# Strassen's weight sums cut into 256 KB chunks, one with each weight piece, and one difference of weights taken on VectorE

## The chip, the cores and the metric

The kernel runs on one core of a Trainium2 chip, as one launch. The metric is the device time of that launch in microseconds, the median of several runs. The core has five engines with instruction streams of their own: TensorE (PE, matrix products), VectorE (DVE), ScalarE (ACT), GpSimd (POOL) and SyncE (SP). Transfers between DRAM and the on-chip memory are issued by SP, ACT and POOL and carried out by 16 DMA engines that all queues share. An engine works its stream in order; an instruction that waits on a semaphore holds up those behind it on the same engine.

## The reference

A two-layer backbone over 256 latent tokens and 256 context tokens of width 2048: first a bidirectional retention layer, then a windowed attention layer, each behind an RMS norm and a modulation ("adaLN") computed from the conditioning vector. The change touches the end of the retention layer and what is prepared for it:

```python
def project(h):
    p = h @ w_in
    q = _heads(p[..., :RET_QK_W], RET_HEADS, RET_DK).astype(jnp.float32) * (RET_DK ** -0.5)
    k = _heads(p[..., RET_QK_W:2 * RET_QK_W], RET_HEADS, RET_DK).astype(jnp.float32)
    v = _heads(p[..., 2 * RET_QK_W:2 * RET_QK_W + RET_V_W], RET_HEADS, RET_DV).astype(jnp.float32)
    g = p[..., 2 * RET_QK_W + RET_V_W:]
    return q, k, v, g

def finish(o, g):
    b, h, l, dv = o.shape
    on = o * lax.rsqrt(jnp.mean(o * o, axis=-1, keepdims=True) + EPS)
    on = on.transpose(0, 2, 1, 3).reshape(b, l, h * dv) * norm_gain.astype(jnp.float32)
    return (on.astype(g.dtype) * jax.nn.silu(g)) @ w_out
```

`w_in` has 2048 x 12288 elements and `w_out` 4096 x 2048, all float32.

## The kernel before

**Precision.** A float32 operand is split into a high half, rounded to the matmul's type, and a low half, the rest. For a weight piece of 512 KB (128 partitions x 1024), `split_w` casts the raw tile `wraw` to `wh` on ScalarE (line 132) and subtracts on VectorE to get `wl` (line 113). The rings of `wraw`, `wh` and `wl` have three buffers each. `mm3` (lines 140 to 142) multiplies high by high, high by low and low by high: 24 matmuls of 512 columns for a piece.

**Stages.** Up to about 150 us the adaLN vectors of the first part and the normed inputs are made. Then come the eight heads (to about 1280 us): for each head the gate, query/key and value products with 24 weight pieces in all, loaded by SP, with the score and output products of a head, its decay table `dd` (a power on GpSimd, L761), its squares (`ossq`, L814), its `rs` (L241) and the sums `ue` of its result (L828) worked in between. The finished head's parts go to DRAM as `uB_d` by transfers issued on ScalarE (L832, L834). The output projection `@ w_out` follows as one level of Strassen's method: seven products of half size, M4 and M1 in one stage (about 1270 to 1385 us), then M5, M7, M2, M3 and M6 (to about 1630 us). The attention layer ends at 2050 us.

**Strassen's weights.** M5, M7, M2 and M3/M6 need sums of two quarters of `w_out` or a quarter itself. The four sums (`SUMS`) are made in DRAM, in the buffer `wS_d`, while the heads run: a job copies 1 MB of the first quarter to `wS_d` (L317, issued on ScalarE), and the step after it adds 1 MB of the second quarter by an accumulating transfer (L323, issued on GpSimd in packets of 4 KB). In front of each accumulating transfer stands the "pin", a copy of one column of the newest `wl` into `pin_t` (L321): GpSimd waits there until that `wl` is made, which fixes when the transfer starts, and the pin holds that `wl` buffer until it has run. `tc.issue_after(x)` places what it encloses behind the instruction x in the issue order. There are 32 jobs, four sums of 4 MB by parts of 1 MB with one more step at the end. `hook()` runs after each weight piece of the heads and takes a step at certain pieces only: its condition on `n`, the count of pieces from 1 to 168, gives six steps up to n = 32 (12, 14, 16, 28, 30, 32), then five in each 24 pieces (four of them two pieces apart, one ten pieces on), and the rest from n = 163.

**adaLN loads.** From n = 33 each hook also takes two adaLN steps (`ADAN`): SP loads 256 KB (`abraw`, four buffers), and VectorE multiplies and sums it with the conditioning rows (`ajunk`, L696), one or two instructions per load.

**M4 and M1.** M4 takes the quarter `wo0[1,1]`, M1 the difference `wo0[0,0] - wo0[1,1]`, which isn't among the sums. `weights1` makes it piece by piece: it loads b, splits it, writes -b into a second raw tile on ScalarE (L1014), and adds the other quarter to that tile by an accumulating transfer issued on GpSimd (L1015); then it splits the tile. In these stages the raw tiles rotate through seven buffers. `merged` (L960, L961) takes a finished product from PSUM into `x1` on ScalarE and VectorE, `prep` loads the next operands back from `uB_d`.

Of the kernel before, what the change touches and what calls it, by code (L numbers as in the profile page):

```python
# [13 lines left out]
AF = mybir.ActivationFunctionType  # L14
ALU = mybir.AluOpType
# [36 lines left out]
def backbone(ctx: ExitStack, tc, xT_d, w0_d, wo0_d, w1_d, wo1_d, adaS_d, adaB_d,  # L52
             crow_d, vec_d, cst_d, ropeR_d, ropeA_d, out_d, dbg=None):
    nc = tc.nc
# [74 lines left out]
    def split_w(raw):  # L129
        wh = strm.tile([P, 2, 512], F32R, name="wh", tag="wh", bufs=3)  # L130
        wl = strm.tile([P, 2, 512], F32R, name="wl", tag="wl", bufs=3)
        last_hi[0] = nc.scalar.copy(wh, raw).ins  # L132
        last_lo[0] = sub(wl, raw, wh).ins
        last_wl[0] = wl
        return wh, wl
# [8 lines left out]
    def gemm_ws(w_d, chunk, nkp, moving, n, hook=None, pre=None, tail=1):  # L144


        accs = [acc_tile()[:, :n] for _ in range(4)]
        w = {}
        for kp in range(nkp):
            if pre is not None:  # L150
                pre(kp)
            w[kp] = load_w(w_d[chunk, kp])
            if kp < nkp - tail:
                kps = [kp]
            elif kp < nkp - 1:
                continue
            else:
                kps = range(nkp - tail, nkp)
            for j in range(4):
                for kb in [2 * k + k2 for k in kps for k2 in range(2)]:  # L160
                    wh, wl = w[kb // 2]
                    js = slice(j * P, (j + 1) * P)
                    mm3(accs[j], (wh[:, kb % 2, js], wl[:, kb % 2, js]), moving(kb),
                        start=(kb == 0), stop=(kb == 2 * nkp - 1))
            if hook is not None:
                hook()
        return accs

    def gemm_ws2(w_d, chunk, nkp, s, hook=None, pre=None, tail=1):
# [4 lines left out]
        for kp in range(nkp):  # L174
            if pre is not None:
                pre(kp)
            w[kp] = load_w(w_d[chunk, kp])
            if nkp - tail <= kp < nkp - 1:
                continue
            kps = [kp] if kp < nkp - 1 else list(range(nkp - tail, nkp))  # L180

            def passes(js_, lo):
                for j in js_:
                    js = slice(j * P, (j + 1) * P)
                    for kb in [2 * k + k2 for k in kps for k2 in range(2)]:
                        wk = w[kb // 2][lo][:, kb % 2, js]
                        if lo:
                            nc.tensor.matmul(accs[j][:, 0:L], lhsT=wk, rhs=h1(kb, s)[:, 0],  # L188
                                             start=False, stop=(kb == 2 * nkp - 1))
                        else:  # L190
                            nc.tensor.matmul(accs[j], lhsT=wk, rhs=h1(kb, s).rearrange("p a t -> p (a t)"),  # L191
                                             start=(kb == 0), stop=False)


            for js_ in ([range(4)] if kp < nkp - 1 else [[j] for j in range(4)]):
                for lo in range(2):
                    passes(js_, lo)
            if hook is not None:
                hook()
        return accs  # L200

    def gemm_ts(w_d, chunk, nkp, stat, ntok, hook=None, pre=None):

        accs = [acc_tile() for _ in range(ntok)]
        for kp in range(nkp):
            if pre is not None:
                pre(kp)
            wh, wl = load_w(w_d[chunk, kp])
            for t in range(ntok):
                for k2 in range(2):  # L210
                    kb = 2 * kp + k2
                    mm3(accs[t], stat(kb, t), (wh[:, k2, :], wl[:, k2, :]),
                        start=(kb == 0), stop=(kb == 2 * nkp - 1))
            if hook is not None:
                hook()
        return accs
# [82 lines left out]
    def pump(n=1):  # L299
        for _ in range(n):  # L300
            if tasks and getattr(tasks[0], "need", None) not in missing:
                tasks.pop(0)()
# [5 lines left out]
    wS_d = dram.tile([4, 4, 4, P, 4, 256], F32, name="wS_d")  # L308
    SUMS = (((1, 0), (1, 1)), ((1, 0), (0, 0)), ((0, 0), (0, 1)), ((0, 1), (1, 1)))

    def sum_jobs():
        todo = [(i, r, slice(2 * q, 2 * q + 2)) for i in (2, 3, 0, 1) for r in range(4) for q in range(2)]
        for n in range(len(todo) + 1):
            if n < len(todo):
                i, r, q = todo[n]
                with tc.issue_after(last_hi[0]):
                    nc.scalar.dma_start(out=wS_d[i, r, q], in_=wo0_d[(*SUMS[i][0], r, q)])  # L317
            if n:
                i, r, q = todo[n - 1]

                pin = nc.gpsimd.tensor_copy(pin_t, last_wl[0][:, 0, 0:1].bitcast(F32)).ins  # L321
                with tc.issue_after(pin):
                    nc.gpsimd.dma_start(out=wS_d[i, r, q], in_=wo0_d[(*SUMS[i][1], r, q)], accum_op=ALU.add,  # L323
                                        max_dma_last_dim=4096)
            yield
    x1_d = dram.tile([KB, P, L], F32, name="x1_d")
# [331 lines left out]
    def raw_tile():  # L658
        i = ring[ring_n[0] % len(ring)]
        ring_n[0] += 1  # L660
        if i is None:
            return strm.tile([P, 2, 512], F32, name="wraw", tag="wraw", bufs=3)
        n, i = i
        return (r1 if n == "H" else top["pool"]).tile([P, 2, 512], F32, name="wraw",
                                                      tag=f"hl{i}" if n == "H" else f"t{i}")
# [9 lines left out]
    if True:  # L675
# [4 lines left out]
        def ada_jobs():  # L680
# [26 lines left out]
            open_top("wx")  # L707

        jobs, sums = ada_jobs(), sum_jobs()
        state = {"n": 0}  # L710

        def hook():
            state["n"] += 1
            n = state["n"]

            if n in (12, 14, 16, 28, 30, 32) or 32 < n < 161 and (n - 33) % 24 in (8, 10, 12, 14, 22) or n > 162:
                next(sums, None)
            if state["n"] > 32:
                with tc.issue_after(last_lo[0]):
                    for _ in range(ADAN[(state["n"] - 33) % 24 // 8]):  # L720
                        next(jobs, None)
            pump()
# [200 lines left out]
    with tc.tile_pool(name="pc", bufs=1, side="right") as pc:  # L923
# [9 lines left out]
        def quarter(src, r, kq):  # L933
            t = raw_tile()
            nc.sync.dma_start(out=t.rearrange("p a t -> p (a t)"),
                              in_=src[r, kq].rearrange("p k c -> p (k c)"))
            return t

        def comb(out, a, b, op):
            return nc.vector.tensor_tensor(out=out, in0=a, in1=b, op=op)  # L940
# [68 lines left out]


        def weights1(r, kq):
            b, a = quarter(wo0_d[1, 1], r, kq), raw_tile()
            yield split_w(b)
            nc.scalar.activation(a, b, AF.Copy, scale=-1.0)  # L1014
            nc.gpsimd.dma_start(out=a.rearrange("p a t -> p (a t)"),  # L1015
                                in_=wo0_d[0, 0, r, kq].rearrange("p k c -> p (k c)"), accum_op=ALU.add)
            yield split_w(a)

        def done1(r, m, accs, n1, n2):
# [37 lines left out]
        def hook_m2(r, kq):  # L1057
            if kq == 1:
                prep(M6, two(r))
            if kq == 2:  # L1060
                residual(two(r + 3), 0)

        stage((M4, M1), weights1, done1, hook1)
        single(M5, wS_d[2], done_m5, hook_m5)
        single(M7, wS_d[3], done_m7, hook_m7)
# [86 lines left out]
    with tc.tile_pool(name="pe", bufs=1, side="right") as pe:  # L1152
# [143 lines left out]
        for ch in ORDER:  # L1296
            c = int(ch[1])
# [128 lines left out]
```

## Time and profile before

| | us |
|---|---|
| median of 3 runs | 2042.59 |
| the runs | 2042.2 to 2047.46 |
| the profiled execution | 2052.4 |
| its span | 2050.6 |
| TensorE busy | 1970.6 |
| VectorE busy | 1323.2 |
| ScalarE busy | 771.4 |
| GpSimd busy | 387.3 |

The mean granted TensorE clock of that execution is 0.985 of full speed. In the rows of the profile an arrow out<-in names a tile written and the tile read; "x32" is a count; a bracket behind a timeline row gives the time the engine stood idle before the instruction and what ended it; "PEld" are TensorE's weight loads; SPq and POOLq are the issuing side of an engine. In a row by stretch the granted clock stands behind the engines' busy times, then the mean busy share of the 16 DMA engines and the GB/s.

### The profile page before, as it was taken

How to read it: one execution, taken by the hardware profiler on the slowest of the kernel's cores; microseconds unless marked ns; L12 is line 12 of the kernel's file. 1: busy time of each engine (PE TensorE's matmuls, PEld its weight loads, DVE VectorE, ACT ScalarE, POOL GpSimd, SP SyncE). 2: the span in 40 equal slices, each digit the busy share in tenths (PEclk: the TensorE clock that was granted, in tenths of full speed). 3: DMA queues.
4: the chain of work that ended last, by engine and by line, in shares of the span. 5: the costliest groups of instructions: out<-in, count | busy, mean ns of one | idle time of the engine just before them, and what ended most of it. 6: DMA issues, size and time to landing. Idle time of an engine off the chain costs nothing. (4 is left out here: it accounts for less than half of the span.)

```text
span 2050.6 us, 26254 instructions
## 1 busy us (share of the span) xinstructions
PE 1970.6 (96%) x9589; PEld 1626.8 (79%) x9589; DVE 1323.2 (65%) x2502; ACT 771.4 (38%) x1147; POOL 387.3 (19%) x207
## 2 busy tenths in 40 slices
PE   6999999999999989999989999979999999999999
PEld 3678787878878877878878878768888888888888
DVE  5575223869859858868547643547778854777765
ACT  4243222223223223223213234445555533666653
POOL 0226524303303302503400201210000010000001
PEclk9999999999999999999999999989999999999999
DMA  9953647797697696697697456768777334444455
GB/s 377 411 202 113 165 144 209 236 305 233 205 305 226 207 304 210 207 302 236 207 312 236 165 157 178 166 151 277 268 245 239 132 108 138 149 134 145 144 188 171
DMA packets 149825, 436.15 MB, mean 213 GB/s; under 512 B 15104, under 2 KB 37952, under 8 KB 145472
## 3 DMA queue, kind: packets, MB, share of 16 engines
q1 hardware_dynamic: 118800, 338.49, 48.5%
q0 software_dynamic: 11008, 41.95, 10.9%
q10 hardware_dynamic: 19888, 54.04, 7.4%
q8 instruction: 75, 1.23, 0.2%
q14 instruction: 54, 0.44, 0.1%
HBM read 416.04 MB, written 85.49 MB: 245 GB/s over the span
## 5 line engine op out<-in xcount | busy, mean ns | idle before, releaser
L113 DVE TENSOR_TENSOR wl<-wraw,wh 128x1024 fp32r<-128x1024 f32 x416 | 510.7, 1232 | 365.5 <-ACT wh L132 355.5
L132 ACT CAST wh<-wraw 128x1024 fp32r<-128x1024 f32 x415 | 433.1, 1050 | 792.6 <-DMA wraw<-in_w 182.9
L696 DVE SCALAR_TENSOR_TENSOR ajunk<-abraw,crow 128x512 bf16<-128x512 f32 x448 | 342.3, 764 | 127.5 <-DMA abraw<-in_adaB 118.8
L142 PE MATMUL acc<-hT_h,wl 128*128 128x512 f32 x928 | 368.2, 397 | 22.0 <-DVE wl L113 22.0
L140 PE MATMUL acc<-hT_h,wh 128*128 128x512 f32 x928 | 367.8, 396 | 6.5 <-ACT wh L132 6.5
L141 PE MATMUL acc<-hl,wh 128*128 128x512 f32 x928 | 365.8, 394 | 0.0
L142 PE MATMUL acc<-wh,hl 128*128 128x512 f32 x704 | 275.9, 392 | 0.0
L140 PE MATMUL acc<-wh,hT_h 128*128 128x512 f32 x576 | 224.6, 393 | 5.8 <-ACT wh L132 3.0
L141 PE MATMUL acc<-wl,hT_h 128*128 128x512 f32 x576 | 226.2, 393 | 3.6 <-DVE wl L113 3.6
L142 PEld LDWEIGHTS acc<-hT_h,wl 128*128 128x128 f32 x928 | 177.2, 191 | 65.2 <-DVE wl L113 27.8
L140 PEld LDWEIGHTS acc<-hT_h,wh 128*128 128x128 f32 x928 | 177.4, 191 | 44.6 <-ACT wh L132 7.8
L141 PEld LDWEIGHTS acc<-hl,wh 128*128 128x128 f32 x928 | 177.0, 191 | 36.2
L761 POOL TENSOR_TENSOR dd<-two,dd 128x128 f32<-128x128 f32 x8 | 168.3, 21038 | 92.0 <-DVE dd L759 92.0
L142 PEld LDWEIGHTS acc<-wh,hl 128*128 128x128 f32 x704 | 132.9, 189 | 27.8
L241 POOL TENSOR_TENSOR rs<-ms,mhalf 128x4 f32<-128x4 f32 (+1 forms) x23 | 32.1, 1397 | 558.4 <-DVE ms L235 310.6
L140 PEld LDWEIGHTS acc<-wh,hT_h 128*128 128x128 f32 x576 | 108.7, 189 | 31.6 <-issue 5.7
L141 PEld LDWEIGHTS acc<-wl,hT_h 128*128 128x128 f32 x576 | 109.0, 189 | 26.9 <-DVE wl L113 5.0
L321 POOL COPY pin_t<-wl 128x1 f32<-128x1 f32 x32 | 16.4, 513 | 472.2 <-DVE wl L113 472.2
L955 PE MATMUL acc<-r_h,wh 128*128 128x512 f32 x240 | 69.4, 420 | 15.2 <-ACT wh L132 10.8
L828 POOL TENSOR_TENSOR ue<-sg 128x512 f32<-128x512 f32 x38 | 66.3, 1759 | 77.9 <-DVE sg L818 44.3
L140 PE MATMUL acc<-wh,hl 128*128 128x512 f32 x192 | 75.4, 393 | 0.0
L141 PE MATMUL acc<-wl,hl 128*128 128x512 f32 x192 | 74.8, 389 | 0.0
(265 smaller groups left out, 2855.3 us busy)
## 6 DMA issues: line engine op xcount, KB each, us to landing
wraw<-in_w SPq DMA_DIRECT2D x272, 512.0 KB, 4.2
abraw<-in_adaB SPq DMA_DIRECT2D x256, 256.0 KB, 4.7
wS_d<-in_wo POOLq DMA_DIRECT2D x32, 1024.0 KB, 12.6
wraw<-in_wo SPq DMA_DIRECT2D x64, 512.0 KB, 4.4
wraw<-wS_d SPq DMA_DIRECT2D x64, 512.0 KB, 4.4
araw<-in_adaS SPq DMA_DIRECT2D x28, 1024.0 KB, 12.9
wraw<-uB_d SPq DMA_DIRECT2D x20, 512.0 KB, 4.4
uB_d<-ue ACTq DMA_DIRECT2D x38, 256.0 KB, 3.4
```

The source lines that it names most:

```text
L113: return nc.vector.tensor_tensor(out=out, in0=a, in1=hi.bitcast(F32), op=ALU.subtract)
L132: last_hi[0] = nc.scalar.copy(wh, raw).ins
L140: nc.tensor.matmul(ps, lhsT=ah, rhs=bh, start=start, stop=False, skip_group_check=skip)
L141: nc.tensor.matmul(ps, lhsT=ah, rhs=bl, start=False, stop=False, skip_group_check=skip)
L142: return nc.tensor.matmul(ps, lhsT=al, rhs=bh, start=False, stop=stop, skip_group_check=skip).ins
L241: nc.gpsimd.tensor_tensor(out=rs, in0=ms, in1=mhalf.to_broadcast([P, n]), op=ALU.pow)
L321: pin = nc.gpsimd.tensor_copy(pin_t, last_wl[0][:, 0, 0:1].bitcast(F32)).ins
L696: nc.vector.scalar_tensor_tensor(out=junk, in0=raw, scalar=1.0, in1=crow[:, t, q * 512:(q + 1) * 512], op0=ALU.mult, op1=ALU.mult, accum_o ...
L761: nc.gpsimd.tensor_tensor(out=dd, in0=two.to_broadcast([P, P]), in1=dd, op=ALU.pow)
L828: (nc.vector if now else nc.gpsimd).tensor_tensor(out=ue, in0=x, in1=y, op=op)
L955: nc.tensor.matmul(accs[j], lhsT=wk, rhs=b, start=(kq == 0 and k == 0), stop=False)
```

## The change

The sums are cut into 128 jobs of 256 KB (64 of the 128 rows of one 512 KB piece, index `x`); an accumulating transfer follows its copy three steps later, not one; and a step is taken at every hook from n = 3 on, until the 131 steps are done (n = 133). In `weights1` both quarters are loaded, and VectorE subtracts in place. The rest is as before.

```diff
     def sum_jobs():
-        todo = [(i, r, slice(2 * q, 2 * q + 2)) for i in (2, 3, 0, 1) for r in range(4) for q in range(2)]
-        for n in range(len(todo) + 1):
+        todo = [(i, r, q, slice(64 * x, 64 * x + 64)) for i in (2, 3, 0, 1) for r in range(4) for q in range(4)
+                for x in range(2)]
+        for n in range(len(todo) + 3):
             if n < len(todo):
-                i, r, q = todo[n]
+                i, r, q, x = todo[n]
                 with tc.issue_after(last_hi[0]):
-                    nc.scalar.dma_start(out=wS_d[i, r, q], in_=wo0_d[(*SUMS[i][0], r, q)])
-            if n:
-                i, r, q = todo[n - 1]
+                    nc.scalar.dma_start(out=wS_d[i, r, q, x], in_=wo0_d[(*SUMS[i][0], r, q, x)])
+            if n >= 3:
+                i, r, q, x = todo[n - 3]
 
                 pin = nc.gpsimd.tensor_copy(pin_t, last_wl[0][:, 0, 0:1].bitcast(F32)).ins
                 with tc.issue_after(pin):
-                    nc.gpsimd.dma_start(out=wS_d[i, r, q], in_=wo0_d[(*SUMS[i][1], r, q)], accum_op=ALU.add,
+                    nc.gpsimd.dma_start(out=wS_d[i, r, q, x], in_=wo0_d[(*SUMS[i][1], r, q, x)], accum_op=ALU.add,
                                         max_dma_last_dim=4096)
             yield
...
-            if n in (12, 14, 16, 28, 30, 32) or 32 < n < 161 and (n - 33) % 24 in (8, 10, 12, 14, 22) or n > 162:
+            if 2 < n:
                 next(sums, None)
...
         def weights1(r, kq):
-            b, a = quarter(wo0_d[1, 1], r, kq), raw_tile()
+            b, a = quarter(wo0_d[1, 1], r, kq), quarter(wo0_d[0, 0], r, kq)
             yield split_w(b)
-            nc.scalar.activation(a, b, AF.Copy, scale=-1.0)
-            nc.gpsimd.dma_start(out=a.rearrange("p a t -> p (a t)"),
-                                in_=wo0_d[0, 0, r, kq].rearrange("p k c -> p (k c)"), accum_op=ALU.add)
+            comb(a, a, b, ALU.subtract)
             yield split_w(a)
```

GpSimd's stream around the fourth decay table and the end of the head before it. Before, one sum job stands between `dd` and the three additions of squares, and none among those, `rs` and the five sums `ue`:

```order
L321 COPY pin_t<-wl 128x1
L323 DMA wS_d<-in_wo 256x1024
L761 TENSOR_TENSOR dd<-two,dd 128x128
L321 COPY pin_t<-wl 128x1
L323 DMA wS_d<-in_wo 256x1024
L814 TENSOR_TENSOR ossq<-ossq,osq 128x512 x3
L241 TENSOR_TENSOR rs<-ms,mhalf 128x4
L828 TENSOR_TENSOR ue<-sg 128x512 x5
L321 COPY pin_t<-wl 128x1
L323 DMA wS_d<-in_wo 256x1024
```

Now, with lines one higher, a pin and its transfer (`64x1024`, a quarter of the size) stand behind nearly each of these:

```order
L762 TENSOR_TENSOR dd<-two,dd 128x128
L322 COPY pin_t<-wl 128x1
L324 DMA wS_d<-in_wo 64x1024
L322 COPY pin_t<-wl 128x1
L324 DMA wS_d<-in_wo 64x1024
L322 COPY pin_t<-wl 128x1
L324 DMA wS_d<-in_wo 64x1024
L322 COPY pin_t<-wl 128x1
L324 DMA wS_d<-in_wo 64x1024
L815 TENSOR_TENSOR ossq<-ossq,osq 128x512
L322 COPY pin_t<-wl 128x1
L324 DMA wS_d<-in_wo 64x1024
```

So the pins of the pieces after `dd` are queued behind it, and the squares, `rs` and `ue` are queued behind pins.

ScalarE's stream at the end of the first gate product (around n = 16; `sg` is the gate taken from PSUM). Before, the four evacuations of the gate stand ahead of the next piece's cast, and a copy of 1 MB behind every second cast:

```order
L132 CAST wh<-wraw 128x1024 x2
L317 DMA wS_d<-in_wo 16x16384
L132 CAST wh<-wraw 128x1024 x2
L317 DMA wS_d<-in_wo 16x16384
L744 ACTIVATE sg<-acc 128x512 x4
L132 CAST wh<-wraw 128x1024
```

Now each cast is followed by a copy of 256 KB (16 rows of 4096 elements):

```order
L132 CAST wh<-wraw 128x1024
L318 DMA wS_d<-in_wo 16x4096
L132 CAST wh<-wraw 128x1024
L318 DMA wS_d<-in_wo 16x4096
L745 ACTIVATE sg<-acc 128x512 x3
L132 CAST wh<-wraw 128x1024
L745 ACTIVATE sg<-acc 128x512
L318 DMA wS_d<-in_wo 16x4096
L132 CAST wh<-wraw 128x1024
L318 DMA wS_d<-in_wo 16x4096
```

The evacuations moved behind casts of the next pieces, and a copy's issue stands behind each cast.

ScalarE's stream in the stage of M4 and M1 (`x` is `merged`'s target). Before, negations stand between the casts:

```order
L960 ACTIVATE x_9972<-acc 128x256 x3
L1014 ACTIVATE wraw<-wraw 128x1024
L960 ACTIVATE x_9972<-acc 128x256
L132 CAST wh<-wraw 128x1024
L1014 ACTIVATE wraw<-wraw 128x1024
L132 CAST wh<-wraw 128x1024 x2
L1014 ACTIVATE wraw<-wraw 128x1024
L132 CAST wh<-wraw 128x1024
```

Now casts and evacuations alone are left, and the subtraction stands on VectorE (L941, not shown):

```order
L961 ACTIVATE x_10260<-acc 128x256
L132 CAST wh<-wraw 128x1024
L961 ACTIVATE x_10260<-acc 128x256 x2
L132 CAST wh<-wraw 128x1024
L961 ACTIVATE x_10260<-acc 128x256
L132 CAST wh<-wraw 128x1024 x5
L116 CAST hT_h<-wraw 128x2x256 x2
```

The negations are gone from between the casts, which now stand in the order of the pieces.

## The prediction

> **What bounds the kernel now.** First the page's busy times, DMA queues and chain: they say which engine sets the end and what else is heavily used.
>
> ```profile
> span 2050.6 us, 26254 instructions
> ...
> PE 1970.6 (96%) x9589; PEld 1626.8 (79%) x9589; DVE 1323.2 (65%) x2502; ACT 771.4 (38%) x1147; POOL 387.3 (19%) x207
> ...
> q1 hardware_dynamic: 118800, 338.49, 48.5%
> q0 software_dynamic: 11008, 41.95, 10.9%
> q10 hardware_dynamic: 19888, 54.04, 7.4%
> ...
> PE 31%; ACT 0%; DVE 0%; issue 0%; DMA 0%; ACTq 0%; DVEq 0%
> ```
>
> TensorE (PE) is busy for 96% of the span, and the chain of the last work names no other engine. So nothing can be won except where PE stands still or runs below its clock. Second view, the busy time by stretch, tells where that is: first column the length, second PE's busy time, then, behind the engines, the granted clock and the DMA share.
>
> ```profile
> 225.00:300.00 75.00, 72.80 (x325) 59.82 (x324) 21.44 (x25) 18.94 (x24) 16.99 (x14) 0.98 0.51 148
> 300.00:400.00 100.00, 94.45 (x426) 77.01 (x425) 56.06 (x105) 23.23 (x27) 38.81 (x16) 0.98 0.71 212
> 400.00:560.00 160.00, 154.93 (x695) 127.52 (x695) 125.59 (x286) 42.65 (x60) 45.85 (x23) 0.99 0.82 252
> 560.00:605.00 45.00, 40.28 (x163) 31.90 (x162) 25.08 (x58) 8.79 (x9) 4.12 (x6) 0.92 0.99 294
> 605.00:715.00 110.00, 109.70 (x506) 91.03 (x505) 93.90 (x214) 32.12 (x49) 39.42 (x14) 1.00 0.71 225
> 715.00:870.00 155.00, 146.39 (x647) 120.21 (x647) 117.38 (x266) 38.09 (x54) 41.91 (x20) 0.97 0.80 243
> 870.00:1025.00 155.00, 150.88 (x676) 124.80 (x675) 107.45 (x243) 41.57 (x60) 43.39 (x22) 0.98 0.79 246
> 1025.00:1180.00 155.00, 148.22 (x665) 121.73 (x665) 88.95 (x181) 41.56 (x64) 20.23 (x17) 0.99 0.75 236
> 1180.00:1270.00 90.00, 87.78 (x402) 72.80 (x401) 36.86 (x57) 34.92 (x52) 8.64 (x8) 1.00 0.57 165
> 1270.00:1385.00 115.00, 98.35 (x489) 83.20 (x488) 55.73 (x68) 54.85 (x73) 20.73 (x20) 0.90 0.69 165
> 1385.00:1440.00 55.00, 55.00 (x314) 48.33 (x313) 39.81 (x51) 32.36 (x46) 0.00 (x0) 0.99 0.83 279
> ```
>
> In the heads (225 to 1270 us) length minus busy time gives 2.2 + 5.55 + 5.07 + 4.72 + 0.3 + 8.61 + 4.12 + 6.78 + 2.22 = 39.6 us of standing. Busy time multiplied by what the clock lacks of 1 (.02, .02, .01, .08, 0, .03, .02, .01, 0) gives another 17.0 us. Together **57 us**. In the first Strassen stage (1270 to 1385) it is 16.65 + 0.10 x 98.35 = **26.5 us**. Between the stalls, and behind 1385, PE has none (109.70 of 110; 55.00 of 55). So 83 us are all that this change can reach. The pair 560:605 and 605:715 shows the kind of place: the loss falls where the DMA share is 0.99.
>
> Third view, the timeline of such a place (GpSimd's sum job, VectorE, PE; start and duration in us, in brackets the idle time before and what ended it), and the sum of VectorE's waits of that kind (us, times, longest):
>
> ```profile
> 583.66 0.88 POOL L323 DMA_DIRECT2D wS_d<-in_wo  x1
> ...
> 596.89 0.69 DVE L696 SCALAR_TENSOR_TENSOR ajunk<-abraw,crow 128x512 bf16<-128x512 f32 x1 [7.70 <-DMA abraw<-in_adaB]
> ...
> 597.51 1.22 DVE L113 TENSOR_TENSOR wl<-wraw,wh 128x1024 fp32r<-128x1024 f32 x1
> ...
> 593.05 0.39 PE L140 MATMUL acc<-hT_h,wh 128*128 128x512 f32 x1
> ...
> 594.63 0.39 PE L141 MATMUL acc<-hl,wh 128*128 128x512 f32 x1
> 598.78 0.80 PE L142 MATMUL acc<-hT_h,wl 128*128 128x512 f32 x1 [3.76 <-DVE wl L113]
> 599.37 0.63 PE L140 MATMUL acc<-hT_h,wh 128*128 128x512 f32 x1
> ```
>
> ```profile
> DVE ajunk L696 <- DMA abraw<-in_adaB: 118.8, 36, 7.9
> ```
>
> A 1 MB accumulate starts at 583.66, and the adaLN load that VectorE wants next lands only at 596.89. VectorE works in order: it stands 7.70 us for this load, the low half `wl` of the next weight piece is queued behind it, PE stands 3.76 us, and afterwards its matmuls take 0.63 us instead of 0.39. A stall costs about its own length once more in the clock.
>
> **The change part by part.**
>
> *The chunks, in the heads.* From the queue rows the DMA time per MB is 48.5% x 2050.6 / 338.49 = 2.94 us of all 16 engines on q1, 5.33 us on q0 (accumulates) and 2.8 us on q10 (copies). A hook with adaLN work loads 0.524 MB of weight and 0.524 MB of adaLN, 3.08 us. PE needs 24 matmuls x 0.226 us (seven starts from 593.05 to 594.63) = 5.42 us for it when nothing else is interleaved (a "bare" hook). Before, every second hook adds 1.049 MB of copy and of accumulate, 8.5 us, so 3.08 + 4.27 = 7.35 us in 5.42: 36% too much for the run of 3 or 4 jobs of a head, so the loads fall behind. After, each hook adds 0.262 MB of both, 0.74 + 1.40 = 2.14 us: 5.22 us in 5.42, 96%, and a mean hook is longer (a head's 155 us less some 7 of loss, over 24 hooks, 6.2 us: 84%). No backlog builds up. A load also stands behind a quarter of a megabyte of copy at most, not a whole one.
>
> What remains of the 57 us: the last head's 2.2 us (no adaLN there; partly another order on ScalarE, whose gain I don't count), 0.6 us at `rs`, and, since 96% is close to full and head ends write `uB_d` as well, I keep one stall with its clock in each of four heads, 4 x 2 = 8 us. So **-46 us**.
>
> *What the heads pay.* 96 more pins and issues on GpSimd and 96 more copy issues on ScalarE:
>
> ```profile
> L321 POOL COPY pin_t<-wl x32: 173/512/2519, 225.3 to 1201.8; 128x1 f32<-128x1 f32 x32
> ...
> L323 POOL DMA_DIRECT2D wS_d<-in_wo x32: 867/880/1107, 225.4 to 1204.3; - x32
> ...
> L317 ACTq DMA_DIRECT2D wS_d<-in_wo x32: 496/504/615, 201.3 to 1180.5; - x32
> ...
> L761 POOL TENSOR_TENSOR dd<-two,dd x8: 20767/20864/21722, 142.9 to 958.1; 128x128 f32<-128x128 f32 x8
> ```
>
> GpSimd: 96 x (0.51 + 0.88) = 133 us, spread over 131 hooks, on an engine that is 19% busy; ScalarE: 96 x 0.50 = 48 us, on one 38% busy. Both lie beside PE; I cost them at 0. Uncovered they would delay a piece by 0.5 us at each hook, against buffers for three pieces. The exception is the 20.9 us decay table `dd`: the pins of the next pieces queue behind it, and each pin holds a `wl` buffer of a ring of three. A pin that waits 20.9 us holds `wl` for the time of 3.8 bare hooks; during `dd` the score products are interleaved, so PE uses up only about three pieces. I take 0, with 4.6 us per head (20.9 - 3 x 5.42) as the bound.
>
> On ScalarE the new copies also stand ahead of the gate evacuations L745 of the first head, behind the casts of two more pieces; what 225 to 300 us lost (2.2 us and 1.5 of clock, with the four evacuations ahead of the cast that PE waited for) should go. It is part of the 57.
>
> *The first Strassen stage.* Each of the 16 pairs loses an ACT negation (1.06 us), the GpSimd accumulate and its landing, and gains a plain 512 KB load and a subtraction on VectorE:
>
> ```profile
> L1014 ACT ACTIVATE wraw<-wraw x16: 1041/1058/1087, 1258.8 to 1378.1; 128x1024 f32<-128x1024 f32 x16
> ...
> PE acc L955 <- ACT wh L132: 11.0, 5, 4.6
> ...
> PE acc L955 <- DVE x L961: 4.3, 3, 3.4
> ...
> PE pm L255 <- POOL rs L241: 2.1, 2, 1.5
> ...
> L113 DVE TENSOR_TENSOR wl<-wraw,wh 128x1024 fp32r<-128x1024 f32 x416 | 510.7, 1232 | 365.5 <-ACT wh L132 355.5
> L132 ACT CAST wh<-wraw 128x1024 fp32r<-128x1024 f32 x415 | 433.1, 1050 | 792.6 <-DMA wraw<-in_w 182.9
> ...
> wraw<-in_wo SPq DMA_DIRECT2D x64, 512.0 KB, 4.4
> ...
> wraw<-in_wo POOLq DMA_DIRECT2D x16, 512.0 KB, 7.5
> ```
>
> Before, a pair is a chain: load 4.4, negate 1.06, accumulate 7.5, cast 1.05, and ScalarE works in order, so that a negation which waits for its load holds up the casts behind it. After, both loads run at once, then 1.23 us on VectorE (the `wl` subtraction has the same shape; I take its time). VectorE gets 16 x 1.23 = 20 us more on 55.73 of 115 us: 66%, beside PE, so 0; uncovered, 20 us. The 11.0 us for `wh` go, with most of the clock's 10 us. What stays of the 26.5: `rs` (1.5 us and as much of clock, 3), the 4.3 us for `x`, whose cause (ScalarE behind a `uB_d` issue) is untouched, with some clock (5.5 together), and 1 for what I can't see. That is **-17 us**.
>
> Sum: -46 - 17 = -63 us against the profiled execution's own 2052.4 us (span 2050.6 and 1.8 around it), so 1989. That execution stands 9.8 us above the median 2042.59 of the runs. If that excess is stall of the removed kind, the gain of a common run is smaller and the time is 1989; if it is there whatever the stalls, 1980. I take **1984 us**, between them.
>
> A rule of the Trainium skill speaks against the change: "DMA: Bandwidth & Descriptors", sections "Rules for kernel authors" and "Bandwidth", wants 1 MiB per DMA and gives a fixed part of about 2.0 us plus bytes over 436 GB/s. By it a 1 MB transfer takes 4.4 us and four quarters 10.4 us, an estimate from that page. The rows below neither need nor decide it.
>
> **Rivals.**
>
> (a) *96% is too full.* If only 0.90 of the DMA time can be used, a bare hook takes 5.22 / 0.90 = 5.80 us; 0.38 us more over some 52 bare hooks is 20 us, with the clock (3 us in each of four heads) 32: **2016 us**. Against it: 0.99 was reached in 560:605.
>
> (b) *Slower: small transfers cost more engine time.* Place: the 101 hooks 33 to 133, each with a copy and an accumulate. In 6.2 us of mean hook stand 3.08 + 0.15 (`uB_d`: 1.3 MB per head at 2.8) and the chunk's 2.14. If chunk time rises by a factor f, the excess is 101 x (3.23 + 2.14 f - 6.2). It outweighs the 63 us from 2.14 f = 3.59, **f = 1.7**. At f = 2 it is +132 us: **2116 us**. The page's 10.4 against 4.4 us would be such a factor, were the fixed part engine time. The rows that bear on it speak against:
>
> ```profile
> abraw<-in_adaB SPq DMA_DIRECT2D x256, 256.0 KB, 4.7
> wS_d<-in_wo POOLq DMA_DIRECT2D x32, 1024.0 KB, 12.6
> ...
> uB_d<-ue ACTq DMA_DIRECT2D x38, 256.0 KB, 3.4
> ```
>
> 256 KB loads make up 67 MB of q1 and the queue still averages 2.94 us per MB; the accumulate's packets are 4 KB (41.95 MB in 11,008) in both kernels. No row shows a 256 KB accumulate; it costs between 0 and 12.6 us to landing, and I take a quarter of the bytes' time.
>
> (c) *Pins behind `dd`.* 4.6 us and the clock's 3.4 at each of six heads, 48 us: **2032 us**, if PE uses the pieces faster than I think.
>
> (d) *The first stage gains nothing*, VectorE being late for `wl` instead of ScalarE for `wh`: 1984 + 17 = **2001 us**.
>
> (e) *No gain in the heads*, the loads being late for another reason (slots freed late by VectorE): 2042.6 - 17 = **2026 us**.
>
> **How the numbers follow.** Forecast 0.64 (1965 to 1997), (a) 0.11, (d) 0.09, (c) 0.05, (e) 0.04, (b) 0.07. If all 83 us went, 2052.4 - 83 = 1969, or 1960 from the median. If the heads keep half and the stage gives 10 us, 2052.4 - 33 = 2019, or 2010 from the median. Range 1960 to 2016, which leaves out (b), (c) and (e). A measurement of this kernel tells about 0.3% (6 us) from no change; (b) between f = 1.6 and 1.8 and a little of (c) and (e) fall within it. Faster 0.89, same 0.04, slower 0.07.
>
> **What would show it.** By stretches, 400 to 1025 us should have PE busy over 0.985 at clock 0.99 or more, with no stretch of DMA share 0.99 and a flat 0.8 to 0.9; the wait of `ajunk` for `abraw` (118.8 us) should fall to a half or less. In the stage of 115 us, about 98 us, PE's 11.0 us for `wh` L132 gone. An `ajunk` wait as large as before in runs of bare hooks means (a); q0 or q10 shares well over 10.9% and 7.4%, (b); PE waiting for `wl` right behind `dd`, (c); PE waiting for `wl` in the stage, (d).

## The result, and the profile after

The changed kernel takes **1972.99 us** (median of 4 runs, 1969.33 to 1973.68) against 2043.88 us before (the three runs shown above and a fourth, 2042.2 to 2047.46): the ratio is 0.9647, 95% interval 0.9629 to 0.9666, 71 us less. Its profiled execution took 1973.68 us, 79 us less than the profiled one before.

The page of the changed kernel, busy times and DMA queues:

```profile
span 1971.8 us, 26838 instructions
...
PE 1940.2 (98%) x9589; PEld 1611.8 (82%) x9589; DVE 1353.4 (69%) x2518; ACT 756.9 (38%) x1131; POOL 476.7 (24%) x383
...
q1 hardware_dynamic: 121104, 346.88, 51.6%
q0 software_dynamic: 10240, 33.56, 9.6%
q10 hardware_dynamic: 22960, 54.05, 8.0%
```

PE's busy time itself fell by 30 us for the same 9589 matmuls: a matmul at the lowered clock counts for longer in "busy" (0.63 us instead of 0.39 in the third view of the prediction), and nearly all of those are gone. GpSimd's busy time rose by 89 us.

Busy time by stretch of the changed kernel (length, PE, PEld, VectorE, ScalarE, GpSimd, clock, DMA share, GB/s); the last row is the first Strassen stage, which begins 48 us earlier than before:

```profile
225.00:300.00 75.00, 75.00 (x349) 62.66 (x348) 20.23 (x22) 19.37 (x24) 28.36 (x40) 1.00 0.76 199
300.00:400.00 100.00, 95.86 (x433) 79.25 (x432) 61.90 (x119) 24.30 (x28) 52.46 (x38) 0.97 0.80 231
400.00:560.00 160.00, 159.97 (x729) 132.89 (x728) 134.37 (x300) 44.80 (x64) 68.98 (x64) 1.00 0.93 280
560.00:715.00 155.00, 154.96 (x706) 128.81 (x705) 129.64 (x288) 41.50 (x58) 67.67 (x62) 1.00 0.92 282
715.00:870.00 155.00, 154.97 (x706) 128.76 (x705) 129.21 (x291) 41.50 (x58) 68.63 (x62) 1.00 0.92 278
870.00:1025.00 155.00, 154.97 (x707) 128.77 (x706) 103.15 (x226) 43.34 (x65) 50.58 (x36) 1.00 0.74 232
1025.00:1180.00 155.00, 155.00 (x713) 129.31 (x712) 90.95 (x174) 50.39 (x77) 14.85 (x9) 1.00 0.46 148
1180.00:1240.00 60.00, 58.83 (x291) 49.57 (x290) 34.85 (x38) 24.06 (x34) 10.24 (x7) 1.00 0.57 190
...
1222.00:1337.00 115.00, 113.27 (x637) 98.51 (x636) 87.55 (x98) 57.31 (x79) 6.11 (x3) 1.00 0.68 221
```

Between 400 and 1025 us PE stands for 0.13 us in all, at a DMA share of 0.92 to 0.93 where the sums run: higher than the 0.80 of before, without its peaks. One stall is left in the heads, in the second row: 4.14 us and 0.03 x 95.86 = 2.9 us of clock. It lies between 335 and 352 us, where the kernel before stood too (3.28 us of these 17, at a clock of 0.90). By the reckoning of the prediction the heads lose 8 us (57 before) and the stage 1.7 us (26.5 before): 74 us of the 79 that the two profiled executions differ by; where the other 5 went isn't shown.

PE's waits, and three of VectorE's (us, times, longest):

```profile
PE pm L437 <- DMA araw<-in_adaS: 17.6, 4, 16.2
PE acc L140 <- DVE r_l L113: 2.7, 1, 2.7
PE acc L956 <- DVE x L962: 1.5, 2, 0.8
PE acc L142 <- DVE wl L113: 1.4, 1, 1.4
PE acc L956 <- ACT wh L132: 1.2, 1, 1.2
...
DVE d L778 <- DMA rows<-gamT_d: 33.7, 7, 13.0
...
DVE wl L113 <- POOL pin_t L322: 23.6, 6, 6.4
...
DVE ajunk L697 <- DMA abraw<-in_adaB: 12.2, 16, 1.7
```

Apart from the start of the kernel (17.6 us for `araw`, a load that the change doesn't touch) PE waits for hardly anything. VectorE's waits for adaLN loads fell from 118.8 us to 12.2. It waits for other things instead, GpSimd's pins among them, and PE shows only 1.4 and 2.7 us at 343 to 347 us, behind the 13.0 us for the decay rows.

### The profile page after: what moved, and what is told of

Its sections match the earlier page's. It is cut to its first block, busy times and chain, and to the rows that moved or that the text cites. A ratio compares the mean times of both kernels' runs of the same rounds, so it can differ in the third digit from the quotient of the medians.

```text
span 1971.8 us, 26838 instructions
## 1 busy us (share of the span) xinstructions
PE 1940.2 (98%) x9589; PEld 1611.8 (82%) x9589; DVE 1353.4 (69%) x2518; ACT 756.9 (38%) x1131; POOL 476.7 (24%) x383
## 3 DMA queue, kind: packets, MB, share of 16 engines
q0 software_dynamic: 10240, 33.56, 9.6%
## 4 chain that ended last, share of the span: by engine, by line
PE 93%; DMA 4%; issue 1%; DVE 1%; ACT 1%; POOL 0%; SPq 0%; ACTq 0%; DVEq 0%; POOLq 0%
PE acc L140 19%; PE acc L141 19%; PE acc L142 19%; PE acc L956 9%; PE acc L191 5%; PE acc L953 5%; PE acc L188 3%; PE pm L140 3%; PE pm L141 3%; PE pm L142 3%; PE acc L500 2%; DMA araw<-in_adaS 1%; PE pm L437 1%; DMA wraw<-in_wo 1%; PE pm L1268 1%
## 5 line engine op out<-in xcount | busy, mean ns | idle before, releaser
L697 DVE SCALAR_TENSOR_TENSOR ajunk<-abraw,crow 128x512 bf16<-128x512 f32 x448 | 349.5, 780 | 21.0 <-DMA abraw<-in_adaB 12.2
L142 PE MATMUL acc<-hT_h,wl 128*128 128x512 f32 x928 | 362.3, 390 | 1.4 <-DVE wl L113 1.4
L322 POOL COPY pin_t<-wl 128x1 f32<-128x1 f32 x128 | 60.2, 471 | 325.0 <-DVE wl L113 325.0
L324 POOL DMA_DIRECT2D wS_d<-in_wo x128 | 105.8, 845 | 11.1 <-issue 9.6
L815 POOL TENSOR_TENSOR ossq<-ossq,osq 128x512 f32<-128x512 f32 x24 | 37.7, 1569 | 188.9 <-ACT osq L809 188.3
## 6 DMA issues: line engine op xcount, KB each, us to landing
araw<-in_adaS SPq DMA_DIRECT2D x28, 1024.0 KB, 12.6
```

Of the source, the lines that this page charges most:

```text
L142: return nc.tensor.matmul(ps, lhsT=al, rhs=bh, start=False, stop=stop, skip_group_check=skip).ins
L324: nc.gpsimd.dma_start(out=wS_d[i, r, q, x], in_=wo0_d[(*SUMS[i][1], r, q, x)], accum_op=ALU.add, max_dma_last_dim=4096)
L697: nc.vector.scalar_tensor_tensor(out=junk, in0=raw, scalar=1.0, in1=crow[:, t, q * 512:(q + 1) * 512], op0=ALU.mult, op1=ALU.mult, accum_o ...
```

## The experiments

Twelve kernels. Each group shares its runs of the kernel before, so ratios are compared; medians of before in the three groups are 2041.76, 2043.84 and 2042.0 us, so a difference in us between kernels of two groups can be off by a few us.

### The parts alone

**stage_only**: the kernel before with the new `weights1`.

```diff
-            b, a = quarter(wo0_d[1, 1], r, kq), raw_tile()
+            b, a = quarter(wo0_d[1, 1], r, kq), quarter(wo0_d[0, 0], r, kq)
             yield split_w(b)
-            nc.scalar.activation(a, b, AF.Copy, scale=-1.0)
-            nc.gpsimd.dma_start(out=a..., in_=wo0_d[0, 0, r, kq]..., accum_op=ALU.add)
+            comb(a, a, b, ALU.subtract)
```

> The kernel before with the new weights1 alone (both quarters loaded, difference on VectorE); the sums in the heads stay in 1 MB jobs. Theory: the two parts of the change are independent, and the first Strassen stage lost 26.5 us of which a fifth is not its doing, so this alone gains 17 to 24 us: 2020 to 2027 us, ratio 0.988 to 0.992. Rival (the stage's stalls come from the load of the heads before it, which this kernel keeps): within 6 us of before, 2038 to 2050 us.

Measured: 2038.79 us, ratio 0.9985 (0.9971 to 0.9998). The rival's number, but the trace shows another reason than the rival's. By stretch:

```profile
1270.00:1310.00 40.00, 28.36 (x136) 23.59 (x135) 20.28 (x26) 12.57 (x18) 3.13 (x3) 0.83 0.36 119
1310.00:1385.00 75.00, 74.02 (x420) 64.16 (x419) 54.20 (x60) 35.09 (x47) 4.36 (x3) 1.00 0.67 220
```

From 1310 us on the new stage has next to no loss (0.98 of 75 us at full clock). The same row of the kernel before:

```profile
1310.00:1385.00 75.00, 61.19 (x297) 51.75 (x298) 34.12 (x43) 35.51 (x48) 8.64 (x10) 0.87 0.65 152
```

In front of it stands a new hole: 11.6 us and .17 of the clock on 28 us. The timeline of ScalarE and GpSimd there, and PE's waits:

```profile
1288.21 1.05 ACT L132 CAST wh<-wraw 128x1024 fp32r<-128x1024 f32 x1 [3.15 <-PE acc L955]
1294.15 1.14 ACT L116 CAST hT_h<-wraw 128x512 fp32r<-128x512 f32 x2 [4.89 <-DMA wraw<-uB_d]
1295.19 0.59 ACT L808 ACTIVATE osq<-pm 128x512 f32<-128x512 f32 x1
...
1295.92 1.29 POOL L814 TENSOR_TENSOR ossq<-ossq,osq 128x512 f32<-128x512 f32 x1 [50.67 <-ACT osq L808]
```

```profile
PE pm L249 <- POOL ossq L814: 6.0, 1, 6.0
PE acc L955 <- ACT z L909: 4.0, 1, 4.0
```

The last head's last square `osq` is queued on ScalarE behind casts of the first stage and behind a split that waits for a `uB_d` load; the norm, the gate and the rest of the head follow it. In the kernel before this square ran at 1275.84 us, ahead of those casts. The hole costs 11.6 us and 0.17 x 28.36 = 4.8 of the 25 us that the stage itself gains, and the rows put it down to the order of the streams at this one seam.

**sums_only**: the changed kernel with the old `weights1` (the diff above, reversed).

> The changed kernel with the old weights1 (negation on ScalarE, accumulating transfer on GpSimd); the sums in 256 KB chunks with each piece. Theory: the heads gain 50 to 57 us and the stage keeps its 22 to 26 us of loss: 1987 to 1999 us, and the gains of this kernel and of the one with the new weights1 alone add up to the 71 us of the whole change. Rival (the gain of the heads needs the new stage): above 2010 us.

Measured: 1993.13 us, ratio 0.9762 (0.9735 to 0.9789), as expected. So the two parts, each alone, gain 0.15% and 2.4%, and together 3.5%. With the sums in chunks the difference by `weights1` is 20 us; with the old sums it is 3. In the stretches they belong to both gains are there; the hole at the seam between them takes most of one away.

**neg_dve**: sums_only with the negation on another engine; the accumulating transfer stays.

```diff
-            nc.scalar.activation(a, b, AF.Copy, scale=-1.0)
+            nc.vector.tensor_scalar(out=a, in0=b, scalar1=-1.0, scalar2=None, op0=ALU.mult)
```

> The kernel with the 256 KB chunks and the old weights1, but with the negation on VectorE instead of ScalarE; the accumulating transfer on GpSimd stays. Theory 1 (ScalarE, waiting at the negation for a load, held up the casts behind it): most of the stage's loss goes, 1972 to 1982 us. Theory 2 (the chain of load, negation and accumulate is itself too long for the raw buffers): the loss stays, 1987 to 1997 us, as in the kernel with the negation on ScalarE.

Measured: 1996.41 us, ratio 0.9774 (0.9758 to 0.979), the number of theory 2. PE's waits in sums_only and then in neg_dve:

```profile
PE acc L956 <- ACT wh L132: 13.1, 6, 4.9
```

```profile
PE acc L953 <- DVE wl L113: 13.3, 6, 2.7
PE acc L956 <- ACT wh L132: 4.6, 3, 2.5
```

The wait moved with the negation, from ScalarE's `wh` to VectorE's `wl`, and got no smaller. What the new `weights1` removes is the chain of load, negation and accumulating transfer, not work of ScalarE. The run doesn't settle the theory's own reason, that the chain is too long for the buffers. Between 1222 and 1364 us the engine with the negation stands six times for the load in front of it, ScalarE for 27.0 us in sums_only, VectorE for 27.3 us here, and VectorE too has the low halves of other pieces queued behind it. So an engine held up in order, whichever it is, explains both runs as well.

**stage_early**: stage_only with the last two steps of the sums moved to the beginning.

```diff
-            if n in (12, 14, 16, 28, 30, 32) or 32 < n < 161 and (n - 33) % 24 in (8, 10, 12, 14, 22) or n > 162:
+            if n in (8, 10, 12, 14, 16, 28, 30, 32) or 32 < n < 161 and (n - 33) % 24 in (8, 10, 12, 14, 22):
```

> The kernel before with the new weights1 alone, but with the two last steps of the sums at n = 8 and 10 instead of 163 and 164. Theory (with the old sums the new stage's gain was lost again in 1295 to 1310 us, where the last head's last square is queued on ScalarE behind five casts of the first stage; that order comes from the scheduler and changes with the steps at the last head): without that, 2018 to 2030 us. Rival (the new stage alone gains nothing whatever the order): 2035 to 2045 us.

Measured: 2046.31 us, ratio 1.0019 (1.0005 to 1.0034): the rival's side, 1 us above its range; the theory's number is missed.

```profile
1235.00:1295.00 60.00, 50.36 (x208) 39.80 (x207) 29.17 (x42) 18.53 (x29) 13.16 (x10) 0.86 0.49 161
1295.00:1385.00 90.00, 85.30 (x474) 73.61 (x473) 69.36 (x78) 43.35 (x57) 7.92 (x3) 1.00 0.63 205
```

A hole is again in front of the stage, 9.6 us and .14 of the clock, now of several smaller waits (the longest 2.1 us, for `wh`), and it isn't the same one: the last square runs at 1260.7 us, and PE waits 0.5 us for `ossq`. So the two steps at n = 163 and 164 are not what makes a hole there. Nor is it the 1 MB jobs as such, or the old hooks: big_even and small_bursts below keep one or the other with the new `weights1`, and PE is busy for 112.53 and 111.26 of the 115 us from 1270 to 1385 at full clock. What in stage_only and stage_early brings the holes about stays open.

### How much of it is the size, and how much the spread

**big_even**: new `weights1`, jobs of 1 MB as before, one step at every fourth hook.

```diff
-            if n in (12, 14, 16, 28, 30, 32) or 32 < n < 161 and (n - 33) % 24 in (8, 10, 12, 14, 22) or n > 162:
+            if 2 < n and n % 4 == 3:
```

> New weights1, and jobs of 1 MB as before, but one step at every fourth hook from n = 3 to 131, so that the mean load of a hook is that of the changed kernel. Theory A (the mean load over some hooks decides): like the changed kernel, 1970 to 1985 us. Theory B (the size of a job decides: a copy and an accumulate of 1 MB take 8.5 us of all DMA engines at once, and the buffers cover no such gap): most of the heads' loss stays, 2005 to 2025 us, with VectorE waiting for abraw 80 us or more.

Measured: 2051.38 us, ratio 1.005 (1.0028 to 1.0073). Beyond both ranges. PE's longest waits, VectorE's for adaLN loads, and ScalarE's timeline at the worst place:

```profile
PE acc L140 <- ACT sg L744: 29.2, 6, 12.5
...
PE acc L141 <- DVE wl L113: 11.5, 6, 3.5
PE pm L141 <- DVE r_l L113: 10.8, 4, 5.8
...
DVE ajunk L696 <- DMA abraw<-in_adaB: 120.0, 36, 6.5
```

```profile
1049.82 7.59 ACTq L832 DMA_DIRECT2D uB_d<-ue  x5
1057.51 2.06 ACT L744 ACTIVATE sg<-acc 128x512 f32<-128x512 f32 x4 [17.53 <-POOL ue L828]
```

The 120.0 us of `ajunk` say that an even spread alone does not cure the late adaLN loads: with 1 MB jobs they are as late as before. PE feels it: it waits 23.0 us for VectorE's `wl` and `r_l`, 26.7 before. The time is worse than this alone explains, since 29.2 us of PE's waits are another thing: here the gate evacuations `sg` are queued on ScalarE behind the `uB_d` issues of the head before, which wait for `ue` (17.53 us), also at 1058 us, when the sums are done. In all PE stands 56.5 us between 225 and 1270 us (39.6 before), and the gain of the new stage hides it in the total. So the waits behind VectorE answer the question, the total time does not.

**half_mb**: the changed kernel with chunks of 512 KB, one step at every second hook, the accumulate two steps behind.

```diff
-        todo = [(i, r, q, slice(64 * x, 64 * x + 64)) ... for x in range(2)]
+        todo = [(i, r, q, slice(128 * x, 128 * x + 128)) ... for x in range(1)]
...
-            if 2 < n:
+            if 2 < n and n % 2:
```

> The changed kernel with chunks of 512 KB at every second hook (n odd), the accumulate two steps behind: the same mean load per hook. A job takes 4.3 us of all DMA engines at once instead of 2.1. If the job must fit between two pieces (2.3 us spare of 5.4 in a bare hook, plus what the three-deep rings cover), half the size should lie between the changed kernel and the 1 MB jobs, nearer to the former: 1975 to 2000 us. If only 256 KB fits: 2010 us or more. If size did not matter below 1 MB: 1970 to 1977 us.

Measured: 1972.21 us, ratio 0.9661 (0.9626 to 0.9695): the changed kernel's time. VectorE's wait there:

```profile
DVE ajunk L697 <- DMA abraw<-in_adaB: 27.9, 22, 3.4
```

27.9 us lie between 12.2 and 120.0, and PE feels none of it: between 400 and 1025 us it is busy for 624.28 of 625. The third expectation held: below 1 MB the size did not matter. A job of 512 KB takes 4.3 us of the DMA engines and a bare hook has 2.3 us to spare, so a job need not fit beside a single piece. Presumably the rings of buffers carry the excess into the next hook, which has no job; where between 4.3 and 8.5 us that ends isn't measured.

**small_bursts**: new `weights1`, chunks of 256 KB, but four steps at each of the old hooks.

```diff
-            if 2 < n:
-                next(sums, None)
+            if n in (12, 14, 16, 28, 30, 32) or 32 < n < 161 and (n - 33) % 24 in (8, 10, 12, 14, 22) or n > 162:
+                for _ in range(4):
+                    next(sums, None)
```

> New weights1, and chunks of 256 KB, but four steps at a time at the hooks at which the kernel before took one (an accumulating transfer follows its copy by four steps, so the times of both are those of before). Theory A (the load per hook decides): the heads' stalls come back, 2010 to 2030 us. Theory B (the size of a transfer decides): the stalls stay away, 1970 to 1985 us.

Measured: 2049.82 us, ratio 1.0037 (1.0019 to 1.0055): theory A's side, 20 us beyond it. The 256 KB by themselves bring nothing: PE stands 56.6 us between 225 and 1270 us, more than the 39.6 of before, and only the gain of the new stage makes the times alike. Why four chunks at a time do worse than one job of 1 MB stays open. ScalarE at one of the bursts:

```profile
560.09 14.83 ACTq L318 DMA_DIRECT2D wS_d<-in_wo  x4
575.01 1.04 ACT L132 CAST wh<-wraw 128x1024 fp32r<-128x1024 f32 x1 [16.96 <-DMA abraw<-in_adaB]
```

Issuing four copies took 14.83 us, and the cast of the next piece was queued behind it. The profile ends ScalarE's idle time with the landing of an adaLN load; what held the issues themselves it doesn't say. In these 15 us the DMA share is 1.05, and SP's issues of three adaLN loads take 10.71 us. This could have been the whole reason, which the next kernel tests.

**small_bursts_pool**: the same, with the copies issued on GpSimd, each behind a pin.

```diff
-                with tc.issue_after(last_hi[0]):
-                    nc.scalar.dma_start(out=wS_d[i, r, q, x], in_=wo0_d[(*SUMS[i][0], r, q, x)])
+                pin = nc.gpsimd.tensor_copy(pin_t, last_wl[0][:, 0, 0:1].bitcast(F32)).ins
+                with tc.issue_after(pin):
+                    nc.gpsimd.dma_start(out=wS_d[i, r, q, x], in_=wo0_d[(*SUMS[i][0], r, q, x)])
```

> As the kernel with four chunks at a time at the old hooks, but the copies too are issued on GpSimd, each behind a pin, so that ScalarE, where four copies took 14.8 us to issue with a cast of weights behind them, is free of them. Theory C (the copies' issue on ScalarE blocked the casts): the heads' stalls mostly go, 1973 to 2000 us, with ScalarE's waits for abraw (170 us) gone. Theory A (the load of the burst on the DMA engines makes the adaLN and weight loads late): they stay, 2010 to 2045 us, as waits of VectorE for abraw.

Measured: 2051.57 us, ratio 1.0036 (1.0019 to 1.0053), 6 us above theory A's range. The waits of the two kernels, first with copies on ScalarE, then on GpSimd:

```profile
ACT wh L132 <- DMA abraw<-in_adaB: 170.4, 13, 18.7
...
DVE ajunk L697 <- DMA abraw<-in_adaB: 53.6, 25, 4.7
```

```profile
DVE ajunk L698 <- DMA abraw<-in_adaB: 102.7, 44, 5.4
...
ACT wh L132 <- DMA abraw<-in_adaB: 4.6, 1, 4.6
```

ScalarE's wait is gone and the time is the same: VectorE now stands 102.7 us for the same loads, and ScalarE 134.3 us for weight pieces (5.5 in small_bursts). The doubled number of pins isn't the reason: VectorE waits 7.4 us for them. The loads are late because of the burst, whoever issues it; theory C fell.

**double_rate**: two steps at each hook from n = 33.

```diff
-            if 2 < n:
-                next(sums, None)
+            if 32 < n:
+                next(sums, None)
+                next(sums, None)
```

> The changed kernel with two steps at every hook from n = 33 on (none before), so 66 hooks carry all 256 KB chunks at twice the rate. Theory (the sum of DMA time per hook decides): 3.08 + 0.15 + 4.28 = 7.5 us in a mean hook of 6.2 us, 66 x 1.3 = 86 us more than the changed kernel: 2040 to 2080 us, with a DMA share near 1 and PE waiting for late pieces in the stretch 320 to 800 us. Rival (the chunk size alone decides): 1970 to 1985 us.

Measured: 2034.89 us, ratio 0.9957 (0.9939 to 0.9975); 62 us above the changed kernel (theory 86), 5 us below its range.

```profile
400.00:560.00 160.00, 142.49 (x626) 116.80 (x625) 114.90 (x260) 36.89 (x52) 86.25 (x99) 0.95 1.01 310
560.00:715.00 155.00, 136.84 (x595) 111.88 (x594) 107.05 (x250) 37.11 (x54) 80.18 (x94) 0.93 1.01 311
```

This is what the even load looks like when it does not fit: a DMA share of 1.01 and 310 GB/s for some 300 us. In the second row PE loses 18 us and .07 of 137, 28 of 155 us or 18%; the sum, 1.3 us too much in 7.5, gives 17%. Chunks of 256 KB give no protection then. The sum was too large in its count, 66 hooks all taken as full: from 330 us, where the doubled steps begin, to 400 us PE still lost only 1.4 us.

### What is left

**no_sums**: the changed kernel without the steps; M5, M7, M2 and M6 read `wo0_d[0, 0]`.

```diff
-            if 2 < n:
-                next(sums, None)
...
-        single(M5, wS_d[2], done_m5, hook_m5)
+        single(M5, wo0_d[0, 0], done_m5, hook_m5)
```

> The changed kernel without any of the sums' copies and accumulates in the heads; M5, M7, M2 and M6 read a plain quarter of the weights instead of a sum, so their products are left wrong by these sums. Theory (the evenly spread chunks are fully hidden): 1963 to 1974 us, at most the stall near 343 us goes. Rival (the sums still cost PE time, by contention or issue): below 1960 us.

Measured: 1966.84 us, ratio 0.9622 (0.9599 to 0.9646), as expected: the 67 MB that the sums copy and add cost about 6 us beside the rest. (Each of the four sums has 8 MB, 32 jobs of 1 MB in all, not the 4 MB that the description of the kernel before gives.) This kernel leaves the sums out, so it tells the time only.

**half_gap**: half_mb without the steps at n = 31, 33 and 35.

```diff
-            if 2 < n and n % 2:
+            if 2 < n and n % 2 and n not in (31, 33, 35):
```

> The kernel with 512 KB chunks at every second hook, without the steps at n = 31, 33 and 35, around the 2 MB load of the conditioning rows (crow) at n = 33. Theory (the last stall of the heads, near 345 us, is that load's, with the decay rows and the casts late behind it, made longer by the sums): 1966 to 1971 us, PE's 2.7 us wait at 345 us at 1 us or less. Rival (it has nothing to do with the sums): unchanged, 1970 to 1975 us, with the 2.7 us still there.

Measured: 1969.9 us, ratio 0.9643 (0.962 to 0.9667), in the theory's range but not to be told from the changed kernel by time. The stretch around the last stall, in the changed kernel, in half_mb, which has those three steps, and here:

```profile
335.00:352.00 17.00, 12.86 (x45) 9.80 (x44) 11.47 (x24) 7.54 (x8) 16.48 (x6) 0.81 0.68 199
```

```profile
335.00:352.00 17.00, 14.34 (x57) 11.37 (x57) 12.90 (x28) 8.65 (x9) 16.57 (x5) 0.90 0.62 212
```

```profile
335.00:352.00 17.00, 16.00 (x76) 13.14 (x75) 14.82 (x32) 7.56 (x9) 13.17 (x1) 1.00 0.52 170
```

Against half_mb, the kernel without this one edit, 2.66 us of standing became 1.00 and the clock stays at full speed; without any sums (no_sums) it is 0.87. So most of the stall comes from the sums' steps at this place. That they do it by delaying the 2 MB load of the conditioning rows fits, since the kernel before stood here too, but isn't shown apart.

**lag_one**: the changed kernel with the accumulate one step behind its copy.

```diff
-        for n in range(len(todo) + 3):
+        for n in range(len(todo) + 1):
...
-            if n >= 3:
-                i, r, q, x = todo[n - 3]
+            if n >= 1:
+                i, r, q, x = todo[n - 1]
```

> The changed kernel with the accumulating transfer one step behind its copy, as before, instead of three. Copies of 256 KB land 5.0 us after their issue, a hook is 5.4 us or longer: theory (the lag is not what helps): 1970 to 1978 us. Rival (GpSimd waits for copies, and its pins hold back the low halves): 1985 us or more, with PE waiting for wl behind pin_t.

Measured: 1978.0 us, ratio 0.9684 (0.9666 to 0.9702): at the edge of the theory's range, 5 us above the changed kernel, or 7 by the ratios. VectorE's wait for pins, PE's for `wl`, and GpSimd at the place:

```profile
DVE wl L113 <- POOL pin_t L322: 32.8, 6, 17.2
...
PE acc L141 <- DVE wl L113: 3.0, 1, 3.0
```

```profile
142.98 41.86 POOL L762 TENSOR_TENSOR dd<-two,dd 128x128 f32<-128x128 f32 x2 [44.12 <-DVE dd L760]
184.80 0.18 POOL L322 COPY pin_t<-wl 128x1 f32<-128x1 f32 x1
```

The first accumulates come two hooks earlier, so the pins of earlier pieces stand behind the first two decay tables (41.86 us): VectorE cannot write `wl` for 17.2 us, and PE stands 3.0 us. In the changed kernel the first pins stand behind the same tables, but VectorE waits at most 6.4 us and PE not at all: between 130 and 225 us it is busy for 95.00 of 95 us, here for 91.98 at a clock of 0.98. That is rival (c), alive at one place, for about 5 us.

## Why the prediction was right

- **What bounds the kernel**: right. Nearly all of the gain, 74 of 79 us, is standing and lowered clock of PE: 57 and 26.5 us of it before, 8 and 1.7 after. The stretches carry this reading; the chain that the prediction also named covers 31% of the span. "About its own length once more in the clock" fits the stall it was read from but is too much as a mean: the prediction's own rows give 17.0 us of clock beside 39.6 of standing.
- **The heads, -46 us**: they gained 49. The mechanism holds in every run with jobs below 1 MB: late adaLN loads at 7.35 us of DMA time in 5.42 of PE (small_bursts_pool keeps that load with small chunks and keeps the stalls), no stalls at 5.22 in 5.42 (half_mb, over two hooks, and the changed kernel). The exception is big_even, for which see the next point. The 8 us kept for one stall in each of four heads were too careful: there was none. But the 7 us at 343 us, which the prediction took as gone with the rest, stayed.
- **The chunk**: the prediction put the gain down to the load per hook, and the size only to a smaller copy ahead of a load. big_even shows that this is half of it: with the same mean load, jobs of 1 MB kept VectorE's 120 us of waits. An even spread and a job below 1 MB were both needed here, and 512 KB was small enough.
- **ScalarE and GpSimd at 0**: right. GpSimd's busy time rose by 89 us; its pins made VectorE wait 23.6 us, none of which reached PE, whose only waits between 150 and 1222 us are 1.4, 2.7 (both near 345 us, behind the decay rows) and 1.2 us (for `rs`). lag_one shows how near the limit this is.
- **The first stage, -17 us**: the term that was mis-sized. It gained 25 in the profiles, and 20 in the comparison of sums_only with the whole. The 5.5 us kept for `x` were 1.5, and the wait for `rs` (1.2 us) lies in front of the stage now. The reason was right in part: I had put it on ScalarE, which works in order; neg_dve shows that the loss follows the negation to another engine. Whether the waiting in order or the length of the chain decides stays open.
- **Own time or median**: the profiled execution of before stood 9.8 us above the median then shown, that of the changed kernel 0.7. This fits the first of the two readings, that the excess is stall of the removed kind, and so 1989; with one profile of each kernel it is not proved. From 1989 to the 1973 measured are 16 us: 3 that the heads and 8 that the stage gave beyond the forecast, and 5 that the stretches don't place. The 1984 on record came nearer to the result than 1989 only because it leaned half way to the other reading. That part is luck; the gain was forecast too small, 63 us of the profiled execution's 79.
- **Rivals**: (a) 0.93 of the DMA engines' time was used without a stall. (b) From the queue rows a MB of accumulate took 9.6% x 1971.8 / 33.56 = 5.64 us against 5.33, of copy 2.92 against 2.8: f = 1.05, not 1.7. The Trainium skill gives the fixed part of about 2.0 us per DMA in "DMA: Bandwidth & Descriptors", section "Anatomy of one DMA — SWDGE (gpsimd) path", and says there that it is dominated by completion latency. These rows agree: four times as many transfers took nearly the same engine time per MB. (c) is lag_one's 5 us. (d) and (e) did not occur.

## What to carry to other kernels

Background traffic is to be reckoned per slot of the foreground: the DMA time of everything that is due in one weight piece against PE's time for that piece. Here the job had to be cut and the jobs spread over all slots: 1 MB jobs spread evenly and 256 KB jobs in bursts both kept the loads late. How small is small enough was found by running it (512 KB did as well as 256), not by the spare time of one slot. A chain of load, small operation, accumulating transfer and cast in front of each piece was better replaced by two plain loads and one operation on an engine with room. And where two changes meet at a seam between stages, their effects need not add up: measure them together and apart.

## What the runs showed of the hardware

An accumulating transfer of 256 KB lands 6.6 us after its issue where 1 MB took 12.6, but costs the engines nearly the same per MB. Where the 16 DMA engines are full (share 1.01) this mix of loads, copies and accumulates moves 310 GB/s. And the issue of a copy can hold an engine for longer than its usual 0.5 us: four copies in a row kept ScalarE's queue for 14.83 us in small_bursts, at a DMA share of 1.05.
